# A new order of 31 DMA transfers, with the last four tiles' transposes taken off PE, in a matmul kernel whose DMA queue is full

## Chip, cores, metric

One core of one Trainium2 chip. The time is the device time of the core in microseconds (us), the median of several runs; a profiled run also has a span, from its first to its last instruction, which is some 1.8 us shorter. A run counts as fast or slow by its clock and its time.

## The reference

```python
x: (16, 512, 1024) float32;  weight: (1024, 768) float32;  scale: 0.1
add_value: (16, 512, 768) float32
return (scale * np.matmul(x, weight) + add_value).astype(np.float32)
```

As the kernel sees it: 8192 rows in 64 tiles of 128. Each tile needs 0.5 MiB of x and 0.375 MiB of add_value, and gives 0.375 MiB of output.

## The kernel before

One list gives all transfers in order: kind (x load, weight, add_value, output), first tile, number of tiles. One engine's queue (SyncEngine, SP) issues them in that order, and a transfer that has to wait holds back all behind it.

```python
STREAM = [
    ("x", 0, 3), ("w", 0, 2), ("w", 2, 2), ("w", 4, 2), ("x", 3, 1), ("w", 6, 2),
    ("a", 0, 3), ("x", 4, 4), ("a", 3, 1), ("a", 4, 4), ("x", 8, 4), ("x", 12, 4),
    ("x", 16, 4), ("a", 8, 8), ("x", 20, 4), ("x", 24, 8), ("o", 0, 8), ("a", 16, 8),
    ("x", 32, 8), ("a", 24, 8), ("a", 32, 8), ("x", 40, 8), ("o", 8, 8), ("x", 48, 8),
    ("a", 40, 8), ("o", 16, 8), ("x", 56, 8), ("a", 48, 8), ("o", 24, 8), ("o", 32, 8),
    ("a", 56, 8), ("o", 40, 8), ("o", 48, 8), ("o", 56, 4), ("o", 60, 1), ("o", 61, 1),
    ("o", 62, 1), ("l", 63, 1), ("r", 63, 1),
]
X_SLOTS = 16      # x tiles in SBUF: x 32-39 lands where tiles 16-23 were
A_SLOTS = 32      # add_value and result share a slot: add_value 32-39 waits for store 0-7
MOVED_ACT  = [14, 18, 22, ..., 58]     # pairs of tiles whose transposition is prepared on ACT
MOVED_POOL = [16, 20, 24, ..., 56]     # and on POOL
```

A moved pair is cast and rearranged by 16 instructions on ACT or POOL and turned by one DVE instruction, `turn_moved`. Other tiles are cast on POOL and transposed on PE. What matters below is the place of these in one step of the loop, since each engine works in this order (cut, with comments added here):

```python
def step():
    t = done["step"]
    ...
            if j == KJ // 2:
                if t + 1 not in in_pair:
                    transpose(t + 1)                      # on PE
                cast_to(min(t + AHEAD, done["x"] - 1))    # AHEAD = 4; on POOL
                for a in range(4):                        # a quarter of a pair each
                    if in_pair.get(t + 8 - a) == t + 8 - a:
                        move_pair(t + 8 - a, a)           # on ACT or POOL
            product(t, j, BOTH)                           # 16 matmuls on PE in all
        finish(t, BOTH[0], 0, N)                          # scale and add, DVE
        if in_pair.get(t + 4) == t + 4:
            turn_moved(t + 4)                             # DVE
    ...
```

## Time and profile before

| | |
|---|---|
| Time | 210.12 us (209.95 to 210.92, 4 runs) |
| Span of the profiled run | 208.5 us, clock 0.96 |
| Bytes | 87.03 MB on the one data queue, 98.2% of the time of 16 DMA engines |
| PE, ACT, POOL, DVE busy | 87, 62, 60, 49% |

In the busy rows of the profile each digit is a fortieth of the span, in tenths. The lines themselves are in the prediction. When each transfer landed can also be read from the semaphore increments in the trace, 16 for each transfer, one by each DMA engine; the landing is the last of them. These are the "landings" below.

### The profile page before, as it was taken

What the parts mean: (1) busy time and instruction counts of PE and PEld (TensorE: products, weight loads), DVE (VectorE), ACT (ScalarE), POOL (GpSimd) and SP (SyncE); (2) the same over time, 40 slices, a digit from 0 to 9 for tenths busy, and PEclk for the clock granted to TensorE, in tenths of its full rate; (3) what the DMA queues carried; (4) which work ended last, traced back from release to release, by engine and by line L of the source; (5) the groups of instructions that cost most, each with busy time, mean ns of one, the idle gap of its engine ahead of it and who ended that gap; (6) DMA issues with size and microseconds to landing.
All of it is one profiled execution on the core that took longest, in us unless ns stands there. A gap on an engine that the chain in (4) does not pass through costs nothing.

```text
span 208.5 us, 2886 instructions
## 1 busy us (share of the span) xinstructions
PE 181.6 (87%) x1096; PEld 110.7 (53%) x1096; DVE 101.3 (49%) x111; ACT 129.0 (62%) x206; POOL 124.3 (60%) x199
## 2 busy tenths in 40 slices
PE   0599399980899997999999999999999999989960
PEld 0455256650466664566666666666666666656630
DVE  0536535511466514855655555555553685233330
ACT  2423000499959798599999999999999900003210
POOL 1310524379898980999998899999999960001000
PEclk9999889996589999999999999999999999999997
DMA  6999999999999999999999999999999999999995
GB/s 236 415 428 440 413 429 434 421 450 406 454 418 448 407 429 462 404 443 420 442 434 413 461 418 424 420 429 437 421 434 424 432 439 424 429 418 439 429 394 214
DMA packets 5629, 87.21 MB, mean 418 GB/s; under 512 B 624, under 2 KB 752, under 8 KB 2032
## 3 DMA queue, kind: packets, MB, share of 16 engines
q1 hardware_dynamic: 5616, 87.03, 98.2%
q8 instruction: 8, 0.13, 0.3%
q14 instruction: 5, 0.04, 0.0%
HBM read 61.87 MB, written 25.17 MB: 417 GB/s over the span
## 4 chain that ended last, share of the span: by engine, by line
DMA 75%; ACT 9%; PE 7%; DVE 3%; SPq 1%; issue 1%; DVEq 0%
DMA out_dram<-ao 35%; DMA ao<-in_add_value_dram 22%; DMA xs<-in_x_dram 13%; ACT va L118 9%; PE mm L177 6%; DMA ao<-in_weight_dram 5%; DVE ao L185 2%; DVE xt L126 1%; PE tp L156 1%; SPq L258 1%; SPq L99 0%; SPq L264 0%; SPq L272 0%; DVEq L185 0%
## 5 line engine op out<-in xcount | busy, mean ns | idle before, releaser
L177 PE MATMUL mm<-w_bf,xt 128*128 128x256 bf16 (+1 forms) x1024 | 173.8, 331 | 8.8 <-DVE xt L164 6.6
L177 PEld LDWEIGHTS <-xt 128*128 128x128 bf16 x1024 | 101.3, 99 | 76.9 <-DVE xt L164 7.0
L118 ACT CAST va<-xs 32x512 bf16<-32x512 f32 x192 | 118.2, 616 | 28.8 <-DMA xs<-in_x_dram 19.1
L118 POOL CAST va<-xs 32x512 bf16<-32x512 f32 x176 | 106.8, 607 | 15.9 <-DVE xt L126 6.2
L185 DVE SCALAR_TENSOR_TENSOR ao<-mm,ao 128x768 f32<-128x768 f32 (+2 forms) x62 | 58.1, 942 | 78.1 <-PE mm L177 49.1
L146 POOL CAST xb<-xs 128x1024 bf16<-128x1024 f32 x15 | 15.2, 1040 | 43.4 <-PE tp L156 22.5
L164 ACT COPY xt<-tp 128x512 bf16<-128x512 bf16 (+1 forms) x11 | 8.2, 785 | 35.3 <-PE tp L156 35.3
L126 DVE STREAM_TRANSPOSE xt<-va 128x1024 f32<-128x1024 f32 x23 | 28.4, 1234 | 0.0
L156 PE MATMUL tp<-identity,xb 128*128 128x128 f32 x72 | 12.9, 314 | 11.2 <-DVE xb L142 7.4
L156 PEld LDWEIGHTS tp<-identity,xb 128*128 128x128 f32 x72 | 9.8, 161 | 13.7 <-issue 7.6
L164 DVE COPY xt<-tp 128x1024 bf16<-128x1024 bf16 x10 | 6.9, 686 | 10.1 <-PE tp L156 10.1
L101 DVE CAST w_bf<-ao 128x768 bf16<-128x768 f32 x8 | 4.1, 556 | 3.8 <-DMA ao<-in_weight_dram 3.8
L142 DVE CAST xb<-xs 128x512 bf16<-128x512 f32 x3 | 1.9, 696 | 6.8 <-DMA xs<-in_x_dram 6.8
L144 POOL CAST xb<-xs 128x512 bf16<-128x512 f32 x2 | 1.6, 834 | 5.5 <-DMA xs<-in_x_dram 5.5
L144 ACT CAST xb<-xs 128x512 bf16<-128x512 f32 x1 | 0.6, 618 | 4.8 <-DMA xs<-in_x_dram 4.8
L213 DVE TENSOR_SCALAR ao<-mm 128x768 f32<-128x768 f32 x2 | 1.8, 952 | 1.9 <-PE mm L177 1.9
L245 DVE TENSOR_TENSOR ao<-ao 128x768 f32<-128x768 f32 x3 | 2.7, 951 | 0.0
L144 ACT ACT_TABLE_LOAD x1 | 1.3, 1283 | 0.7 <-PEq L289 0.7
L210 ACT ACTIVATE ao<-mm 128x768 f32<-128x768 f32 x1 | 0.8, 817 | 0.0
masks.py:197 POOL MEMSET identity<- 128x128 f32 x1 | 0.2, 204 | 0.3 <-POOLq L289 0.3
masks.py:199 POOL TENSOR_SCALAR_AFFINE_SELECT identity<-identity 128x128 f32<-128x128 f32 x1 | 0.3, 292 | 0.1
L289 POOL MEMSET const-float32-0.0<- 128x1 f32 x1 | 0.1, 98 | 0.2 <-issue 0.2
(3 smaller groups left out, 0.3 us busy)
## 6 DMA issues: line engine op xcount, KB each, us to landing
ao<-in_add_value_dram SPq DMA_DIRECT2D x7, 3072.0 KB, 26.1
out_dram<-ao SPq DMA_DIRECT2D x7, 3072.0 KB, 23.9
xs<-in_x_dram SPq DMA_DIRECT2D x5, 4096.0 KB, 18.8
xs<-in_x_dram SPq DMA_DIRECT2D x5, 2048.0 KB, 26.6
ao<-in_weight_dram SPq DMA_DIRECT2D x4, 768.0 KB, 9.6
xs<-in_x_dram SPq DMA_DIRECT2D x1, 1536.0 KB, 6.1
ao<-in_add_value_dram SPq DMA_DIRECT2D x1, 1536.0 KB, 19.3
out_dram<-ao SPq DMA_DIRECT2D x1, 1536.0 KB, 12.9
```

Of the source, the lines that this page charges most:

```text
L101: nc.vector.tensor_copy(w_bf[:, j + i, :], ao[:, s + i, :])
L118: move(moved[t0][32 * b:32 * b + 32, :, a, :], src[32 * a:32 * a + 32, :, b, :])
L126: nc.vector.transpose(xt.rearrange("p i c m -> p (i c m)"), moved.pop(t0).bitcast(fp32).rearrange("p c a k -> p (c a k)"))
L142: nc.vector.tensor_copy(xb[:, 0:K // 2], src[:, 0:K // 2])
L144: other(xb[:, K // 2:K], src[:, K // 2:K])
L146: nc.gpsimd.tensor_copy(xb, src)
L156: nc.tensor.transpose(tp[:, c, :], pairs[:, c * P:(c + 1) * P], identity)
L164: evacuate(xt_tiles[t][:, c:c + q, :].bitcast(bf16), tp[:, c:c + q, :].bitcast(bf16))
L177: nc.tensor.matmul(mm_tiles[t, cols[0]][:, n0:n1], lhs(t, j), w_bf[:, j, n0:n1], start=(j == 0), stop=(j == KJ - 1))
L185: nc.vector.scalar_tensor_tensor(a, mm_tiles[t, part][:, n0:n1], float(scale), a, op0=mybir.AluOpType.mult, op1=mybir.AluOpType.add)
L245: nc.vector.tensor_add(ao[:, t, :], ao[:, EARLY_AT + t, :], ao[:, t, :])
L258: nc.sync.dma_start(xs[:, k:k + n, :], rows(x_v, s, n))
```

## The change

Its intent: fewer and larger transfers, loads and stores in eights, and no transposes on PE from tile 14 on.

```diff
 STREAM = [
     ("x", 0, 3), ("w", 0, 2), ("w", 2, 2), ("w", 4, 2), ("x", 3, 1), ("w", 6, 2),
-    ("a", 0, 3), ("x", 4, 4), ("a", 3, 1), ("a", 4, 4), ("x", 8, 4), ("x", 12, 4),
-    ("x", 16, 4), ("a", 8, 8), ("x", 20, 4), ("x", 24, 8), ("o", 0, 8), ("a", 16, 8),
-    ("x", 32, 8), ("a", 24, 8), ("a", 32, 8), ("x", 40, 8), ("o", 8, 8), ("x", 48, 8),
-    ("a", 40, 8), ("o", 16, 8), ("x", 56, 8), ("a", 48, 8), ("o", 24, 8), ("o", 32, 8),
-    ("a", 56, 8), ("o", 40, 8), ("o", 48, 8), ("o", 56, 4), ("o", 60, 1), ("o", 61, 1),
-    ("o", 62, 1), ("l", 63, 1), ("r", 63, 1),
+    ("a", 0, 8), ("x", 4, 4), ("x", 8, 8), ("a", 8, 8), ("x", 16, 8), ("o", 0, 8),
+    ("a", 16, 8), ("x", 24, 8), ("x", 32, 8), ("a", 24, 8), ("a", 32, 8), ("x", 40, 8),
+    ("o", 8, 8), ("o", 16, 8), ("a", 40, 8), ("x", 48, 8), ("a", 48, 8), ("x", 56, 8),
+    ("o", 24, 8), ("o", 32, 8), ("a", 56, 8), ("o", 40, 8), ("o", 48, 8), ("o", 56, 5),
+    ("o", 61, 3),
 ]
-MOVED_ACT = [..., 58]
-MOVED_POOL = [..., 56]
+MOVED_ACT = [..., 58, 62]
+MOVED_POOL = [..., 56, 60]
     ... the weight's view merged to (r n): the same runs of 6144 B ...
     ... small edits that follow from these (asserts, the choice of the evacuating engine) ...
```

More of the change, by code (lines that the diff above doesn't have):

```diff
@@ L26 @@
 EARLY = 3
-MOVED_ACT = [14, 18, 22, 26, 30, 34, 38, 42, 46, 50, 54, 58]
-MOVED_POOL = [16, 20, 24, 28, 32, 36, 40, 44, 48, 52, 56]
+MOVED_ACT = [14, 18, 22, 26, 30, 34, 38, 42, 46, 50, 54, 58, 62]
+MOVED_POOL = [16, 20, 24, 28, 32, 36, 40, 44, 48, 52, 56, 60]
 @with_exitstack
@@ L67, in rows @@
         return view[:, s // G, s % G:s % G + n, :]
-    w_v = weight.rearrange("(c p r) n -> p c r n", p=P, r=2)
+    w_v = weight.rearrange("(c p r) n -> p c (r n)", p=P, r=2)
     const = ctx.enter_context(tc.tile_pool(name="const", bufs=1))
@@ L95, in load_w @@
         s = A_SLOTS - KJ + j
-        if n == 1:
-            nc.sync.dma_start(ao[:, s, :], w_v[:, j // 2, j % 2, :])
-        else:
-            nc.sync.dma_start(ao[:, s:s + 2, :], w_v[:, j // 2, :, :])
+        assert j % 2 == n % 2 == 0
+        nc.sync.dma_start(
+            ao[:, s:s + n, :].rearrange("p (c r) n -> p c (r n)", r=2),
+            w_v[:, j // 2:(j + n) // 2, :])
         for i in range(n):
@@ L161, in transpose @@
         q = KC // pieces
-        evacuate = nc.scalar.copy if t <= EARLY or t > LAST_PAIR else nc.vector.tensor_copy
+        evacuate = nc.scalar.copy if t <= EARLY else nc.vector.tensor_copy
         for c in range(0, KC, q):
@@ L216, in head @@
             done["step"] = EARLY
-    LAST_PAIR = max(in_pair)
     EARLY_AT = A_SLOTS - KJ - EARLY
@@ L259 @@
             done["x"] = s + n
-            if last < EARLY:
+            if s < EARLY:
                 head(op, s, n)
```

## The prediction

> **What bounds the kernel now.** I read the page first: the busy rows, then the row of the 16 DMA engines over the span, then the queues.
>
> ```profile
> PE 181.6 (87%) x1096; PEld 110.7 (53%) x1096; DVE 101.3 (49%) x111; ACT 129.0 (62%) x206; POOL 124.3 (60%) x199
> ...
> ACT  2423000499959798599999999999999900003210
> POOL 1310524379898980999998899999999960001000
> ...
> DMA  6999999999999999999999999999999999999995
> GB/s 236 415 428 440 413 429 434 421 450 406 454 418 448 407 429 462 404 443 420 442 434 413 461 418 424 420 429 437 421 434 424 432 439 424 429 418 439 429 394 214
> DMA packets 5629, 87.21 MB, mean 418 GB/s; under 512 B 624, under 2 KB 752, under 8 KB 2032
> ...
> q1 hardware_dynamic: 5616, 87.03, 98.2%
> q8 instruction: 8, 0.13, 0.3%
> ...
> DMA 75%; ACT 9%; PE 7%; DVE 3%; SPq 1%; issue 1%; DVEq 0%
> ```
>
> The reader is to see that the DMA engines are full in every slice but the first and last. The one data queue took 98.2% of 16 engines' time, and the chain that ended last is three quarters DMA. PE's 87% comes with holes that cost nothing. A change can gain only by moving the same 87.03 MB in less engine time, and can lose only by letting the queue run dry.
>
> Second, the SyncEngine timeline, which gives the rate. The issue at 122.12 us waited for the landing of store 8-15, the one at 146.37 for store 16-23, the one at 170.86 for store 24-31 (they reuse the stored slots).
>
> ```profile
> 122.12 0.33 SPq L264 DMA_DIRECT2D ao<-in_add_value_dram  x1
> ...
> 146.37 0.33 SPq L264 DMA_DIRECT2D ao<-in_add_value_dram  x1
> ...
> 170.86 0.34 SPq L264 DMA_DIRECT2D ao<-in_add_value_dram  x1
> ```
>
> Between two of these landings lie one x of eight (4.194 MB) and two 3.146 MB transfers: 10.486 MB in 24.25 us, then in 24.49 us, so 432 and 428 GB/s. An x of eight costs 9.70 us, an add_value or store of eight 7.28 us.
>
> Third, the DMA queue's own waits, and POOL and ACT, which release the x slots.
>
> ```profile
> SPq L258 <- ACT va L118: 90.1, 5, 22.0
> SPq L264 <- DMA out_dram<-ao: 40.1, 4, 23.2
> SPq L272 <- DVE ao L185: 21.7, 8, 6.9
> ```
>
> ```profile
> 43.98 2.55 POOL L118 CAST va<-xs 32x512 bf16<-32x512 f32 x4 [0.78 <-DMA xs<-in_x_dram]
> 46.60 1.03 POOL L146 CAST xb<-xs 128x1024 bf16<-128x1024 f32 x1
> 47.70 7.76 POOL L118 CAST va<-xs 32x512 bf16<-32x512 f32 x12
> 56.18 10.36 POOL L118 CAST va<-xs 32x512 bf16<-32x512 f32 x16 [0.72 <-DMA xs<-in_x_dram]
> ```
>
> The issuing engine waits long, yet the DMA row shows no hole: it waits while earlier transfers are still being moved. What decides the changed kernel is whether each issue still comes before the queue is empty. A pair of tiles costs POOL 10.36 us; on ACT 16 casts took 10.03 us.
>
> **What the Trainium skill says.** "DMA: Bandwidth & Descriptors", section "Where 436 GB/s comes from", puts the fabric ceiling at 435 GB/s and the HBM share of one core at about 358. The trace agrees with the first (432 above) and not with the second (417 GB/s of HBM traffic over the span): there is no unused bandwidth. The same page, "Measured (HBM→SBUF, 128 partitions, SWDGE, issued from GpSimd)", advises transfers of at least 1 MiB. That is the obvious hope for this change, but its table times single transfers. In this trace, with a full queue, the packets say otherwise: 32 KB took 1213 ns, 24 KB 912, 16 KB 614, 12 KB 461, 9 KB 352, 3 KB 121, 1 KB 46. That is a straight line plus some 9 ns per packet. "Trace Analysis", section "What "DMA-bound" means", names specific DMA engines first, and large descriptors as the remedy; the trace agrees on the bound, and on the remedy only by those 9 ns. "TensorE: Matmul & The Clock Gate", Part 1, says that a window of 3.4 us idle halves the clock. The trace has that: from 45 to 60 us, with a PE wait of 6.57 us, the granted mean is 0.66. It doesn't set the end.
>
> **The change part by part.**
>
> 1. Fewer packets. 39 transfers become 31, each of 128 data packets and 16 semaphore packets (39 x 16 = 624, the page's count under 512 B). Using the packet times above, in engine time over 16 engines: x goes from five loads in 16 KB packets and five in 32 KB to one and seven: before 128 x (461 + 159 + 5 x 614 + 5 x 1213), after 128 x (461 + 159 + 614 + 7 x 1213), so 3.8 us / 16 = 0.24 us less. The head of add_value: 352 + 121 + 461 becomes 912 ns, times 128, / 16 = 0.18 us. Stores 56-63: 461 + 3 x 121 + 84 + 46 becomes about 573 + 352 (five and three tiles, 15 KB by the line above), 0.23 us. Semaphores: 128 x 9 ns / 16 = 0.07 us. Sum 0.72 us.
>
> 2. The weight view. The page's 752 to 2032 packets between 2 and 8 KB are 1280 = 128 x 10, which fit only if the four weight loads already go as one 6144 B run per partition. So nothing changes: 0.
>
> 3. Pairs 60 and 62 off PE. PE loses 16 transposes (4 x 0.44 us = 1.76 us), ACT loses four copies and gains 10.0 us, POOL swaps four 1.04 us casts for 10.4 us, DVE gains two transposes of 1.23 us. At that time both are idle in the present kernel (the last eight digits of their rows), and PE isn't the bound: 0, if the last store is still in time.
>
> 4. The order. I lay the new list in a row at 9.70 and 7.28 us (smaller ones in proportion), from the weights' end near 15.6 us in the present trace. Landings: add_value 0-7 22.9, x 4-7 27.8, x 8-15 37.5, add_value 8-15 44.8, x 16-23 54.5, store 0-7 61.7, add_value 16-23 69.0, x 24-31 78.7, x 32-39 88.4, add_value 24-31 95.7 and 32-39 103.0, x 40-47 112.7, stores 120.0 and 127.3, add_value 40-47 134.6, x 48-55 144.3, add_value 151.6, x 56-63 161.3, stores 168.6 and 175.9, add_value 56-63 183.2, stores 190.4, 197.7, 202.3 and 205.0. An issue is in time if it comes some 1.35 us before the landing of what precedes it: 1.0 us from issue to first packet (the first issue at 0.74, packets from 1.75) and 0.35 us from last packet to landing (6.44 to 6.79). The tight ones:
>
> - x 32-39 needs slots 16-23 free. POOL must move pairs 16 and 20 after x 16-23 lands, with the cast of tile 13 between (it stands behind the first quarter of pair 16 in POOL's order): 2.6 + 1.1 + 7.8 + 10.4 = 21.9 us. The queue holds 7.28 + 7.28 + 9.70 = 24.3 us behind that landing, less 1.35. Slack 1.0 us: issue at 76.4, needed by 77.4. ACT is done earlier, 20.1 us.
> - x 40-47 needs pairs 24 and 28 moved after 78.7: 2 x 10.36 gives 99.5, needed by 101.7. Slack 2.2 us.
> - x 48-55 (POOL done 120.3, needed by 133) and x 56-63 (141, needed by 150) have over 9 us; add_value 40-47 and 56-63 wait for stores 5.9 us ahead of need.
> - The last store: POOL ends pair 60 near 185.9, its turn on DVE 187.1; finish of 57 at 188.0 frees PSUM; then four tiles at 2.60 us give 198.4, last addition 198.9; needed by 200.9. Slack 2.0 us.
>
> So no hole is expected. The present kernel, laid out the same way, would land its last store at 205.7, and the trace has 207.6: two microseconds come from unevenness among the 16 engines. The eight 16 KB instruction packets each hold one engine for about 1 us, and the 16 increments of a landing, 0.38 us apart in the first transfer, are 2.4 us apart late in the run. PE's program is hardly shorter, so I keep those two microseconds. Net: 210.14 - 0.72 = 209.4 us.
>
> **The rivals.**
>
> A: the queue runs dry at x 32-39, because POOL now starts pair 16 when all of x 16-23 is in (54.5 us) rather than at 43.98 as now. For it: slack of only 1.0 us, and everything behind it in the queue is held. Against: the slack is counted in stable durations (POOL casts 603 to 612 ns), and a delay of the slowest DMA engine adds slack. If it happens I expect 0.5 to 2 us, so 210 to 211.5 us.
>
> B: the longer transfers are worth more than the packet arithmetic: up to 3 us, if the uneven engines come from the small transfers. For: 205.0 against 207.6. Against: the unevenness appears at instruction fetches, not at small transfers. It would give 207 to 208 us.
>
> C: the tail becomes compute-bound, with ACT and POOL late on pairs 60 and 62. For: ACT was full from 86 to 146 us. Against: 2.0 us of slack, and lateness there costs one for one only beyond it: 210 to 213 us if both start 4 us late.
>
> **Range and chances.** The present runs spread from 209.95 to 210.92, so half a microsecond each way is noise. A and C widen upwards, B downwards: 208.4 to 211.2. Faster by over 2% needs 205.9, below even the hole-free, even-engine sum (205.0 + 0.9 to the end of the span + the 1.6 us by which the runs exceed the profile's span = 207.5): 0.01. Slower by over 2% needs some 5 us of holes, several of the slacks failing: 0.04. Within: 0.95.
>
> **What would show it.** Right: DMA digits all 9, data queue packets 4464 (31 x 144), about 97.8 to 98.5% of engine time, x 32-39 issued near 76.4 and landing 9.7 us after x 24-31; PE ahead of now by the middle, with waits on DVE and POOL that move nothing. Wrong by A: a digit under 9 near 77 or 101 us and a landing distance over 10.5 us. By B: all landings evenly earlier. By C: the last store issued after 201 us and the last slices of the DMA row thin.

## The result

The changed kernel took 213.74 us (213.39 to 214.14, 4 runs) against 210.12. The ratio is 1.0165, 95% interval 1.0133 to 1.0197. Ratios here are the mean time of one kernel's fast runs over that of the other's of the same rounds, so not quite the ratio of the medians quoted. The result is slower by 1.65%: inside 2%, but 4.3 us above the predicted 209.4 and outside the range.

The page of the changed kernel, the same rows as shown of before (busy time, the DMA engines by slice, the queue, the chain that ended last):

```profile
PE 180.3 (85%) x1080; PEld 109.0 (51%) x1080; DVE 101.8 (48%) x113; ACT 134.8 (64%) x218; POOL 130.0 (61%) x211
...
DMA  6999999999899979999999999999999999999975
GB/s 227 422 447 422 424 433 458 410 428 483 357 436 449 421 319 384 405 432 435 419 401 388 432 432 436 445 428 416 442 430 432 424 427 436 432 430 418 439 340 229
...
q1 hardware_dynamic: 4464, 87.03, 97.1%
...
DMA 43%; PE 29%; POOL 16%; issue 6%; SPq 2%; DVE 1%; POOLq 0%; DVEq 0%
```

The packets are the 4464 that were predicted, and the bytes are the same. But in the 15th slice (74 to 79 us) and the 16th the engines moved 319 and 384 GB/s instead of some 430. The chain has changed its make-up: DMA fell from 75 to 43%, PE rose to 29 and POOL to 16%. Compute now stands in line with the transfers. The queue's own timeline and POOL's say where:

```profile
60.67 18.57 SPq L256 DMA_DIRECT2D xs<-in_x_dram  x2
79.29 0.90 SPq L262 DMA_DIRECT2D ao<-in_add_value_dram  x2
102.09 0.33 SPq L256 DMA_DIRECT2D xs<-in_x_dram  x1
```

```profile
56.99 2.55 POOL L117 CAST va<-xs 32x512 bf16<-32x512 f32 x4 [9.36 <-DMA xs<-in_x_dram]
59.61 1.03 POOL L145 CAST xb<-xs 128x1024 bf16<-128x1024 f32 x1
60.71 18.18 POOL L117 CAST va<-xs 32x512 bf16<-32x512 f32 x28
81.29 62.46 POOL L117 CAST va<-xs 32x512 bf16<-32x512 f32 x96 [2.41 <-DMA xs<-in_x_dram]
```

The first line of the queue merges two x issues: x 24-31 at 60.67 and x 32-39, which ends the merged piece at 60.67 + 18.57 = 79.24 and, at 0.33 us for an issue, began at 78.91. That is the moment POOL ended pair 20 (60.71 + 18.18 = 78.89). POOL works from 57.0 to 78.9 without a stop; it could start pair 16 only when all eight tiles 16-23 had landed, where the kernel before started it at 43.98. Its last line shows x 24-31 landing at 81.2. So x 32-39 was issued 2.3 us before the landing ahead of it. By the landings it came in at 93.40, 12.23 us after x 24-31 (81.17), where the plain distance is 9.70. The busy time of the DMA engines in the stretch around it (the columns after the engines are PE's clock, the DMA share and GB/s):

```profile
60.00:76.00 16.00, 15.12 (x93) 9.19 (x94) 7.55 (x8) 15.69 (x27) 14.92 (x25) 1.00 1.03 441
76.00:84.00 8.00, 8.00 (x52) 4.80 (x50) 5.08 (x6) 3.45 (x6) 5.25 (x10) 1.00 0.79 297
84.00:125.80 41.80, 39.60 (x235) 23.27 (x233) 21.37 (x22) 40.97 (x68) 38.96 (x65) 0.96 1.01 423
```

I laid all landings against the plain distances (9.70 us for eight x, 7.28 for eight others, in proportion for the rest) and added up the places with more than 0.15 us of delay. Kernel before: 2.2 us late, of which 1.35 at x 8-11, 0.4 at x 24-31 and the rest at add_value 48 and 56. Changed kernel: 5.9 us late, of which 1.25 at x 8-15, 1.1 at x 16-23, 2.5 at x 32-39, 0.7 at x 40-47 and 0.3 at add_value 56. So the two orders differ at x 16-23, x 32-39 and x 40-47.

### The profile page after: what moved, and what is told of

It reads as the page before. It is cut to its first block, busy times and chain, and to the rows that moved or that the text cites. A ratio compares the mean times of both kernels' runs of the same rounds, so it can differ in the third digit from the quotient of the medians.

```text
span 211.8 us, 2865 instructions
## 1 busy us (share of the span) xinstructions
PE 180.3 (85%) x1080; PEld 109.0 (51%) x1080; DVE 101.8 (48%) x113; ACT 134.8 (64%) x218; POOL 130.0 (61%) x211
## 3 DMA queue, kind: packets, MB, share of 16 engines
q1 hardware_dynamic: 4464, 87.03, 97.1%
## 4 chain that ended last, share of the span: by engine, by line
DMA 43%; PE 29%; POOL 16%; issue 6%; SPq 2%; DVE 1%; POOLq 0%; DVEq 0%
DMA xs<-in_x_dram 32%; PE mm L176 27%; POOL va L117 15%; DMA out_dram<-ao 11%; PE tp L155 2%; POOL xb L145 1%; SPq L96 1%; DVE ao L184 1%; SPq L256 1%; SPq L262 0%; POOLq L145 0%; POOLq L117 0%; DVE xt L125 0%; DVEq L184 0%
## 5 line engine op out<-in xcount | busy, mean ns | idle before, releaser
L117 ACT CAST va<-xs 32x512 bf16<-32x512 f32 x208 | 128.1, 616 | 41.8 <-DMA xs<-in_x_dram 39.3
L117 POOL CAST va<-xs 32x512 bf16<-32x512 f32 x192 | 116.5, 607 | 26.5 <-DMA xs<-in_x_dram 18.2
L184 DVE SCALAR_TENSOR_TENSOR ao<-mm,ao 128x768 f32<-128x768 f32 (+2 forms) x62 | 56.5, 926 | 30.3 <-PE mm L176 25.3
L125 DVE STREAM_TRANSPOSE xt<-va 128x1024 f32<-128x1024 f32 x25 | 30.9, 1234 | 45.4 <-POOL va L117 45.4
L145 POOL CAST xb<-xs 128x1024 bf16<-128x1024 f32 x11 | 11.2, 1040 | 29.0 <-DMA xs<-in_x_dram 25.4
L155 PE MATMUL tp<-identity,xb 128*128 128x128 f32 x56 | 10.2, 318 | 17.9 <-POOL xb L145 10.2
L155 PEld LDWEIGHTS tp<-identity,xb 128*128 128x128 f32 x56 | 7.6, 163 | 20.1 <-POOL xb L145 10.9
L163 ACT COPY xt<-tp 128x512 bf16<-128x512 bf16 (+1 forms) x7 | 4.1, 656 | 8.0 <-PE tp L155 8.0
```

Source lines behind the costliest of these rows:

```text
L117: move(moved[t0][32 * b:32 * b + 32, :, a, :], src[32 * a:32 * a + 32, :, b, :])
L125: nc.vector.transpose(xt.rearrange("p i c m -> p (i c m)"), moved.pop(t0).bitcast(fp32).rearrange("p c a k -> p (c a k)"))
L145: nc.gpsimd.tensor_copy(xb, src)
L155: nc.tensor.transpose(tp[:, c, :], pairs[:, c * P:(c + 1) * P], identity)
L163: evacuate(xt_tiles[t][:, c:c + q, :].bitcast(bf16), tp[:, c:c + q, :].bitcast(bf16))
L184: nc.vector.scalar_tensor_tensor(a, mm_tiles[t, part][:, n0:n1], float(scale), a, op0=mybir.AluOpType.mult, op1=mybir.AluOpType.add)
```

## The experiments

Theory D: the loss is the queue running dry before x 32-39. Rivals: P, packets of this order are slow by themselves or at random; T, PE's unbroken last 16 tiles set the end. "Lead" below is the time from an issue to the landing of the transfer ahead of it; "loss" is the distance from that landing to its own, less the plain distance. Both come from the trace of each run. The last engine's landing is only one of 16; where the text says "by the mean", the mean of a transfer's 16 increments is taken instead. Ratios are to the kernel before, on the same chip.

### The changed kernel again

> The changed kernel once more, unchanged, as the yardstick of this group. Theory D (the queue runs dry before x 32-39, because POOL frees slots 16-23 too late): again 1.6 to 1.7% slower than before, x 32-39 landing about 12.2 us after x 24-31 where 9.7 would do. Rival P (packets of the x loads are slowed at random by something outside the order): the place and size of the lateness move from run to run.

Measured: 214.36 us (212.96 to 214.64), ratio 1.0187 (1.0144 to 1.0231). x 32-39 had a lead of 2.2 us and a loss of 2.8 us; x 16-23 lost 1.4. The places of the loss repeat, so they aren't random. One thing differed: the last store lost 1.3 us here and none in the first profile.

### More work in the queue ahead of x 32-39

```diff
-("x", 24, 8), ("x", 32, 8), ("a", 24, 8), ("a", 32, 8),
+("x", 24, 8), ("a", 24, 8), ("x", 32, 8), ("a", 32, 8),
```

> The changed kernel with one swap: add_value 24-31, which waits for nothing, is issued ahead of x 32-39, so 7.3 us more of work lie in the queue while POOL finishes. Theory D: the distance from the landing ahead of x 32-39 to its own is back at 9.7 us, and the kernel gains the 2.5 us: about 211.2 us. Rival P: unchanged at 213.7. Rival T (the end is set by PE's unbroken last 16 tiles and not by the queue): the hole goes but the time stays within 0.5 us of 213.7.

Measured: 213.05 us (212.44 to 214.63), ratio 1.015 (1.010 to 1.020). The lead of x 32-39 became 9.6 us and its loss went from 2.5 to nothing (9.64 us), as theory D said. The time hardly followed. Its DMA row shows a new thin place further on:

```profile
DMA  6999999999899999999899999999999999999985
GB/s 240 417 455 406 429 442 446 408 437 473 356 425 426 465 408 436 439 442 417 327 467 302 425 442 434 428 456 401 425 468 411 423 434 429 429 423 439 422 368 242
```

The 15th slice is full again, but the 20th and 22nd (from 100 to 105 and 111 to 116 us) moved 327 and 302 GB/s: x 40-47. It was issued at 102.47, as in the changed kernel (102.09), because it waits for POOL's pairs 24 and 28, which start when x 24-31 lands (81 us in both). The transfers ahead of it now landed at 105.8 instead of 108.0. Its lead fell to 3.3 us and it lost 1.8. Most of the gain was given back one x load later.

### x 16-23 in two fours

```diff
-("a", 8, 8), ("x", 16, 8), ("o", 0, 8),
+("a", 8, 8), ("x", 16, 4), ("x", 20, 4), ("o", 0, 8),
```

> The changed kernel with x 16-23 loaded as two fours again, in the same place. POOL can start pair 16 about 4.9 us earlier. Theory D: x 32-39 is issued about 7 us before x 24-31 lands instead of 2.3, the hole is gone, about 211.2 us. Rival P: 213.7. If both this and the swap gain the same 2.5 us, it is the lead of that one issue and neither the size of x 16-23 nor the place of add_value 24-31 as such.

Measured: 213.24 us (213.05 to 213.40), ratio 1.0144 (1.0110 to 1.0179). The same in another way: x 32-39 was issued at 72.99, 8.3 us of lead, no loss; x 40-47 had 3.35 us of lead and lost 3.2. The gain of 2.5 us was expected in the time and didn't come. The expectation was mine, and it overlooked the second short lead. Nor does all of this loss lie at the start of x 40-47. Here are its first stretch and its last:

```profile
102.00:106.00 4.00, 4.00 (x26) 2.38 (x25) 3.68 (x4) 3.93 (x7) 3.72 (x7) 1.00 0.86 309
110.00:115.00 5.00, 4.95 (x32) 3.05 (x32) 2.85 (x4) 4.89 (x9) 4.64 (x9) 1.00 1.04 339
```

In the second stretch the engines are busy throughout and yet move only 339 GB/s. The last packets of x 40-47, just ahead of store 8-15, took longer than such packets take elsewhere, by 1.3 us per engine in sum (1.2 us in the run before this one). More on this at the second swap.

### The opposite dose: less work in the queue

```diff
-("x", 16, 8), ("o", 0, 8), ("a", 16, 8), ("x", 24, 8), ("x", 32, 8), ("a", 24, 8),
+("x", 16, 8), ("a", 16, 8), ("x", 24, 8), ("x", 32, 8), ("o", 0, 8), ("a", 24, 8),
```

> The opposite dose: store 0-7 goes behind x 32-39, so the queue holds 7.3 us less while POOL works. Theory D: x 32-39 is still issued about 22 us after x 16-23 lands, which is now 5 us after x 24-31 has landed; x 32-39 lands some 17 us after x 24-31, and the kernel loses about 5 us more: 218 to 219 us. Rivals P and T: within 1 us of 213.7, since the same bytes move and PE's tiles are not concerned.

Measured: 219.71 us (219.28 to 220.05), ratio 1.0454 (1.0420 to 1.0489). x 24-31 landed at 73.06, x 32-39 was issued at 77.82 and landed at 91.47, 18.4 us later. Theory D holds for this dose; P and T would have left the time alone. The landing came 1.4 us later than expected, and this shows what a start costs: with all engines dry, x 32-39 landed 13.65 us after its issue, 3.95 us more than its packets need, where the prediction's rule allows 1.35. Of the 3.95 us, 1.0 is slow packets just ahead of store 0-7. By the way, x 16-23 lost nothing here (9.71 us): it is the first variant in which a load and not a store follows it.

### Two fine doses on POOL

```diff
+ (nc.vector if i == 13 else nc.gpsimd).tensor_copy(xb, src)       # first: cast of tile 13 on DVE
+ if i == 13: nc.gpsimd.tensor_copy(xb, src)                       # second: done twice on POOL
```

> The changed kernel with one cast, that of tile 13, taken from POOL to DVE, so that POOL frees slots 16-23 about 1.1 us earlier: x 32-39 issued 3.3 us before x 24-31 lands on its last engine, instead of 2.2. Theory D (the hole opens on the DMA engines that are ahead, 2.6 us before the last one lands, so 1.0 us of start and 0.35 us of landing must lie before that: about 4 us of lead are needed): the distance to the landing of x 32-39 falls from 12.2-12.5 to about 11.2 us and the kernel gains about 1.1 us. The prediction's rule (1.35 us before the last landing is enough): no change at all, since the lead was over 1.35 us already.

Measured: 213.28 us (212.71 to 213.68), ratio 1.0134 (1.0101 to 1.0167). Lead 3.28 us and no loss at x 32-39 (9.71 us), where 1.5 was expected; x 40-47, lead 3.5, lost 2.1 instead.

> The changed kernel with the cast of tile 13 done twice on POOL (same result): x 32-39 is issued 1.1 us before x 24-31 lands. Theory D: the distance grows to about 13.4 us and the kernel loses about 1.1 us, one for one. The prediction's rule: only some 0.25 us are lost.

Measured: 215.20 us (214.79 to 215.85), ratio 1.023 (1.0196 to 1.0264). Lead 1.08 us, loss 1.9 at x 32-39, then 0.7 at add_value 32-39 and 1.8 at x 40-47 (lead 5.9). From one to the other 2.2 us of lead moved the time by 1.9 us, though the prediction's rule has only a quarter of a microsecond at stake. POOL's chain is on the path. On the last engine the loss at x 32-39 isn't the one for one that I expected. By the mean it is: x 32-39 lost 1.0 us with the cast on DVE and 3.2 us with the cast done twice, 2.2 us more for 2.2 us less lead.

### Tiles 60 to 63 back on PE, in the new order

```diff
-MOVED_ACT = [..., 58, 62];  MOVED_POOL = [..., 56, 60]
+MOVED_ACT = [..., 58];      MOVED_POOL = [..., 56]
```

> The changed kernel with tiles 60 to 63 back on PE as before. All theories about the order: the hole at x 32-39 stays (12.2 to 12.5 us) and the time stays within 0.5 us of 213.7 to 214.4. A theory that the moved pairs cost time (ACT and POOL late at the end): some 1 us faster. A theory that PE's unbroken last 16 tiles set the end: 1 to 1.8 us slower, as 4 x 0.44 us of transposes come back on PE.

Measured: 215.54 us (214.78 to 215.94), ratio 1.0239 (1.0205 to 1.0273), against 1.0165 and 1.0187 with the pairs moved: some 1.1 to 1.6 us slower by the ratios, though the interval overlaps that of the second measurement (1.0144 to 1.0231). PE's timeline in the changed kernel, then here:

```profile
162.67 43.07 PE L176 MATMUL mm<-w_bf,xt 128*128 128x512 bf16 x256 [4.69 <-DVE ao L184]
```

```profile
162.67 32.50 PE L176 MATMUL mm<-w_bf,xt 128*128 128x512 bf16 x184 [5.73 <-DVE ao L184]
195.01 0.60 PE L155 MATMUL tp<-identity,xb 128*128 128x128 f32 x4
...
204.56 4.06 PE L176 MATMUL mm<-w_bf,xt 128*128 128x512 bf16 x24
```

In both, PE runs without a hole from 162.67 to its end. It ends at 205.7 with the pairs moved and at 208.6 without, and the last store was issued at 206.23 and at 209.11. Of these 2.9 us the transposes explain 1.8 (4 x 0.44 us); the granted clock was also lower here, 0.92 against 0.96 from 162.67 to 195 us. So theory T is true of the new order to this extent: its last tiles have next to no slack, and moving the pairs is what keeps PE just in time. The reason is x 48-55, which the new list puts behind store 16-23 and add_value 40-47. It landed at 150.0 us, in the kernel before at 131.8.

### The kernel before with only the pairs moved

> The kernel before, in its own order, with the pairs 60 and 62 moved off PE as in the change and nothing else. If the order alone makes the difference: within 0.3% of before. If the moved pairs cost by themselves: up to 1% slower.

Measured: 210.39 us (210.15 to 211.10), ratio 0.9995 (0.9962 to 1.0027). In the old order the moved pairs change nothing, so the loss comes with the new list.

### Both short leads mended

```diff
-("x", 24, 8), ("x", 32, 8), ("a", 24, 8), ("a", 32, 8), ("x", 40, 8), ("o", 8, 8),
+("x", 24, 8), ("a", 24, 8), ("x", 32, 8), ("a", 32, 8), ("o", 8, 8), ("x", 40, 8),
```

> The changed kernel with two swaps: add_value 24-31 ahead of x 32-39, and store 8-15 ahead of x 40-47, so that neither x load is issued with less than about 9 us of work before the landing ahead of it. Theory D2 (two issues are short of lead, one after the other; mending the first alone only hands its gain to the second, which waits for POOL's pairs 24 and 28 and comes at 102.2 us in every variant): both x loads land 9.7 to 9.9 us after what precedes them, about 3.3 us less than in the changed kernel, 210.3 us. Rival (x 40-47 is slow by itself, whatever its lead): x 40-47 again 11.5 to 12.9 us, no gain over 213.

Measured: 210.42 us (210.06 to 210.82), ratio 1.0011 (0.9994 to 1.0027). Leads of 9.5 and 10.7 us, distances of 9.72 and 9.63: no loss at either. The whole 3.3 us came back, and the packets ahead of store 8-15 are no longer slow.

```profile
DMA  6999999999999999999999999999999999999994
...
76.00:84.00 8.00, 7.95 (x50) 4.87 (x50) 4.83 (x5) 3.51 (x7) 5.37 (x9) 1.00 0.99 422
```

The DMA row is full from the second slice on, and the stretch that had a share of 0.79 and 297 GB/s has 0.99 and 422. PE's last run starts at 159.50 here, 3.2 us earlier, so the end on PE follows the transfers forward.

### The second swap alone

> The changed kernel with only the second swap: store 8-15 ahead of x 40-47; x 32-39 keeps its short lead of about 2.2 us. Theory D2: x 32-39 again lands 12.2 to 12.5 us after x 24-31 and only the 0.1 to 0.8 us at x 40-47 are saved: about 213.2 us. So neither swap alone is worth over about 1 us, and both together 3.3. If the second swap were the whole cure, whatever the first issue does: 210.4 us.

Its edit is the second half of the one above. Measured: 213.76 us (213.33 to 214.14), ratio 1.0175 (1.0158 to 1.0193). x 32-39, lead 2.2, lost 1.1 (2.2 by the mean), and add_value 32-39, now just ahead of store 8-15, lost another 2.0 with 19.4 us of lead; x 40-47 (lead 13.7) lost nothing. So of the four arrangements, none, the first swap, the second and both, the ratios are 1.0165 and 1.0187, 1.015, 1.0175, and 1.0011: neither alone is worth much, because the other short lead takes over or the same one stays. The sum was right (3.0 us), its place within was not.

The place is worth a look across all profiles. Ahead of store 8-15 packets took 0.2 to 1.3 us per engine more than usual in all nine runs of the new order in which x 32-39 or x 40-47 had a lead of under 3.6 us and this store was the next, and at most 0.05 us in the other runs. With store 0-7 moved directly behind the dry x 32-39, the slow packets (1.0 us) were ahead of that store and not of store 8-15. So in these traces a short lead costs twice, at its start and just ahead of the next store. No run separates the two, and why packets are slow there stays open. To this extent rival P had a point: part of the loss is slow packets in a full queue, but in fixed places, and ahead of store 8-15 only after a short lead (store 0-7 follows below).

### The first store

In most variants of the new order the load ahead of store 0-7 loses 1.1 to 1.4 us. Two runs moved that store.

```diff
-("x", 16, 8), ("o", 0, 8), ("a", 16, 8), ("x", 24, 8),
+("x", 16, 8), ("a", 16, 8), ("o", 0, 8), ("x", 24, 8),                        # changed kernel
+("x", 16, 8), ("a", 16, 8), ("x", 24, 8), ("o", 0, 8),                        # with both swaps
```

> The changed kernel with store 0-7 and add_value 16-23 exchanged, so that x 16-23 is followed in the queue by a load and not by a store. If the 1.1 to 1.4 us that x 16-23 loses in every variant but the one with the store further back come from the store right behind it: x 16-23 lands 9.7 us after add_value 8-15 and the gain is up to 1.1 us, unless it is handed on to x 32-39 and x 40-47, whose leads don't change. If they come from the load's size or place: 10.8 to 11.1 us again.

Measured: 212.90 us (212.84 to 213.42), ratio 1.0136 (1.0117 to 1.0154). x 16-23 lost nothing (9.72 us) and add_value 16-23, now ahead of the store, lost 1.4. The loss goes with the place ahead of the first store, not with the size of the x load, and not with the instruction fetch in x 16-23, which stayed there (54.67 us). Within it the last packets are slow: 22 packets between 59.1 and 60.6 us took 1.0 to 1.7 us instead of 0.91.

> Both swaps, and store 0-7 put behind x 24-31 as well, so that the first store starts some 20 us after its issue and not 8. If the 1.1 to 1.4 us lost by the load ahead of the first store hang on its coming early: x 16-23 9.7 us, x 24-31 9.7 to 10.1 us, and 209.3 to 209.6 us, faster than both kernels. If the loss goes with whatever load is ahead of the first store: it moves to x 24-31, which then lands 10.8 to 11.1 us after add_value 16-23, and the time is that of both swaps, 210.4 us.

Measured: 210.99 us (210.67 to 212.01), ratio 1.0048 (1.0026 to 1.0070). It doesn't answer the question. Store 0-7 no longer fills the queue ahead of x 24-31, whose lead fell to 3.4 us. That load lost 2.9 us, partly in its first packets and partly ahead of the store. I hadn't reckoned with that lead; it is the same mistake once more.

> The version with both swaps once more, as the yardstick of this group: 210.1 to 210.8 us, within 0.3% of before.

Measured: 210.31 us (210.14 to 210.52), ratio 1.0004 (0.9991 to 1.0017). The version with both swaps equals the kernel before.

### All repairs in one

Both swaps, add_value 16-23 ahead of store 0-7, and x 48-55 two places earlier; the second version has x 16-23 in fours on both sides of add_value 8-15 as well.

```diff
-("o", 16, 8), ("a", 40, 8), ("x", 48, 8), ("a", 48, 8),          # both swaps
+("o", 16, 8), ("x", 48, 8), ("a", 40, 8), ("a", 48, 8),
```

> All repairs in one, everything still in eights: add_value 16-23 ahead of store 0-7, add_value 24-31 ahead of x 32-39, store 8-15 ahead of x 40-47, and x 48-55 two places earlier so that PE's last 16 tiles start some 10 us sooner. Theory D2 and the end on PE: no landing distance over the plain one except at instruction fetches, last store no longer waiting for PE, 209.0 to 209.8 us, that is 0.2 to 0.5% faster than before. If packets of eights are slow by themselves: over 211.

Measured: 210.84 us (209.96 to 211.79, 6 runs), ratio 1.0031 (0.9999 to 1.0063).

> The same with x 16-23 in two fours on both sides of add_value 8-15, as in the kernel before, so that POOL starts pair 16 about 13 us sooner and x 32-39 has over 10 us of lead. Same theory: 209.0 to 209.8 us, not distinguishable from the version in eights, because a lead beyond what is needed buys nothing.

Measured: 211.22 us (209.83 to 212.20, 6 runs), ratio 1.0047 (1.0020 to 1.0074).

Both missed the expectation of 209.0 to 209.8; only single runs came near it. The version in eights fell into two groups, three runs at 210.0 and three at 211.6 to 211.8, and the profiled run of each version was its slowest, so what follows explains the slower runs only. In the profiled runs the last store lost 1.5 and 2.5 us, and no x load after x 16-23 lost anything. So the x leads were sound and the end was not. Bringing x 48-55 forward put add_value 40-47 back, to a landing at 146.9 and 146.4 us; DVE's finish of tile 40 waited for it, and PE for DVE:

```profile
148.01 2.72 PE L176 MATMUL mm<-w_bf,xt 128*128 128x512 bf16 x8 [3.04 <-DVE ao L184]
150.95 53.48 PE L176 MATMUL mm<-w_bf,xt 128*128 128x256 bf16 x321 [0.22 <-issue]
```

That is PE in the version in eights. From there it runs unbroken to 204.4 us, where with both swaps alone it ended at 201.3; about 163 us its granted clock also fell, to 0.6 and 0.5 for a slice in the two versions. One wait of PE had been exchanged for another.

No version beat the kernel before beyond its interval.

## Why the prediction was wrong

**What bounds the kernel, and the packets: right.** 4464 packets as predicted. The merged transfers land as the packet times said: add_value 0-7 took 7.30 us, its three parts before 7.46; stores 56-63 took 7.31 us in two, 7.46 in six. The weight view changed nothing. The saving was too small to show in the time, and the version with both swaps, which has all of it, equals the kernel before: the sum of 0.72 us is supported by distances of landings, not by the total.

**The rows and POOL's chain: right.** The prediction had x 32-39 issued 21.9 us after x 16-23 lands; it was 22.0 us (56.94 to 78.91). It had 24.3 us of work behind that landing; there were 24.2.

**The step that failed** is the sentence "An issue is in time if it comes some 1.35 us before the landing of what precedes it". By it, x 32-39 with 2.3 us of lead was safe, and x 40-47 with the 3.3 us that it had in two variants as well. The wait was right and the rule was mis-sized, in two terms.

- The start of a load. The 1.35 us are the time to the first packet of the first engine, and from the last packet to the landing. They leave out that first packets after a pause are slow. The trace that the prediction read has this: the first x load landed 6.05 us after its issue with 8 x 0.461 = 3.69 us of packets per engine, 2.36 us more. With store 0-7 behind x 32-39 all engines were dry, and there the first packets started 1.2 us after the issue on average and took 0.7 us longer than their 1.21; with 0.4 us for the landing that makes 2.3. In the changed kernel the first packets of 15 engines took 1.34 to 2.51 us; by the mean its loss of 2.2 us at x 32-39 is 1.4 us of idle engines and 0.7 us of longer packets.
- The landing to count from. The first engine lands 2.6 us ahead of the last (78.56 and 81.17 for x 24-31), the mean engine 2.0 us ahead, and it is dry that much sooner. I had noted the spread of the landings, and argued that only the last engine counts.

By the mean the sum closes. In all seven runs in which x 32-39 had 1.1 to 3.6 us of lead and a load behind it, it landed 2.3 to 2.7 us plus the plain 9.70 after its issue. Counted from the last landing, about 2.0 us after the mean one, this makes a needed lead of some 4.3 to 4.9 us for a load, an estimate from these runs, where the prediction had 1.35. For the last store, whose data come from SBUF, the rule was right: where its engines were dry it landed, by the mean, 1.3 us plus its plain distance after its issue.

Even the last engine, busy to 80.81, shows its next packet only at 82.73 (matched by ends and starts, since the records don't name the engine). Why a late issue delays also the engine that was not dry is not shown. And x 40-47 lost more than this sum gives, for the greater part in the slow packets ahead of store 8-15. What is shown on the last engine is a bound: in the new order x 32-39 and x 40-47 lost under 0.1 us whenever their lead was 8 us or more, between 0 and 3.2 us with leads of 3.3 to 6.3, and 1.1 to 2.8 with leads of 1 to 2.3. In the kernel before the shortest lead of an x load from x 24 on is 6.0 us (x 48-55), without loss.

**Rival A: right in kind and place, mis-sized.** It put the hole at x 32-39, with 0.5 to 2 us. The loss there was 2.5 to 2.8 us in the two profiles of the changed kernel, of which idle engines are only a part, and with x 40-47 the short leads cost 3.3 us, which both swaps brought back. The second short lead was hidden in the changed kernel behind the first: it costs little only because the first hole has already delayed what is ahead of it.

**The remaining 1 us.** The version with both swaps is still 1.0 us above 209.4. The load ahead of the first store loses 1.3 to 1.4 us in it (0.4 to 0.5 by the mean); in the kernel before the load ahead of the first store (x 24-31) lost 0.4 (0.1). That covers 0.9 to 1.0 us of it by count on the last engine and less by the mean, but no run removed this loss by itself, so it is argued and not shown. Its mechanism stays open.

**The end: the slack of 2.0 us was too large.** The last store was issued at 206.23 us, when its engines were just running out (0.6 us of slack on the landings of the first profile, none in the second). The prediction followed the finish of tile 57 and missed the longer chain: x 48-55, one pair on POOL, 16 tiles on PE. The verdict on the moved pairs, 0, holds in the old order. In the new one they are worth some 1.1 to 1.6 us, with intervals that overlap in part.

**Rivals B and C.** B is out: the engines are no more even (2.6 us apart) with larger transfers. C in its form (ACT and POOL late on pairs 60 and 62) is not what happened; PE was the engine near the limit.

## What to carry to other kernels

When a full queue is issued from one engine in order, list the lead of every issue that waits for compute, and judge it against the DMA engines that are ahead, not the one that is last, and allow for slow first packets: here 2 us of lead cost 2.5 us and 8 us cost nothing. Mending one short lead moves later transfers forward and so shortens the next lead, so mend all of them, and put transfers that wait for nothing ahead of those that wait for compute. Larger transfers delay the moment at which the first of their tiles can be used, and in a queue that is already full they gave nothing that the total time showed.

## What the Trainium skill lacked or had wrong

- "DMA: Bandwidth & Descriptors" has no word on how early the next transfer must be issued to keep the 16 engines busy. Here a lead of 2.2 to 2.3 us cost 1.1 to 2.8 us, with the engines 2.6 us apart; with 8 us or more nothing was lost.
- The same page, "Measured (HBM→SBUF, 128 partitions, SWDGE, issued from GpSimd)", gives 341 GB/s for 1 MB. It doesn't say that the shortfall vanishes in a full queue: in the kernel before, the 1.18 MB of add_value 0-2 landed 2.79 us after its predecessor, which is 423 GB/s.
- The same page, "Where 436 GB/s comes from", says that the HBM side (about 358 GB/s) binds HBM to SBUF transfers. For a core alone that is wrong: the kernel before moved 432 GB/s over 24 us. The section before it gives that figure only for both cores of a pair streaming.
- No page has slow load packets directly ahead of a store: the load ahead of the first store lost 1.1 to 1.4 us on the last engine in most runs of this order, moving with the store from x 16-23 to add_value 16-23; and after a short lead packets ahead of store 8-15 took 0.2 to 1.3 us per engine longer.
- No page has the slow first packets of a load after a pause: 0.7 us per engine on packets of 1.21 us.
- No page gives what instruction fetches take from a full DMA queue: eight 16 KB packets in a run, each about 1.0 us on one engine where a data packet of that size takes 0.61, with a data packet near it some 0.5 us longer.
